# A two-layer decoder trunk on one core: the second chunk's unit 1 ahead of the first chunk's unit 3 in the first output pair

## The chip, the core and the metric

The kernel runs on one core of a Trainium2 chip. Its engines are PE (TensorE, the matmuls; PEld is its weight load), DVE (VectorE), ACT (ScalarE), POOL (GpSimd) and SP (SyncE, which only issues transfers here). The metric is the time of one execution on the device in microseconds (us).

## The reference

Two layers on x of 256 positions by 2048 columns, all in float32, cut to what matters here:

```
for l in range(2):
  h = rms_norm(x, mix_norm[l])
  q, k, v, uv, gate_logits = split(h @ w_in[l])
  branch_a = sliding_window_attention(q, k, v, sinks[l]) @ w_attn_branch[l]
  branch_b = chunked_sgu(gelu(uv), ...) @ w_sgu_branch[l]
  gates = sigmoid(gate_logits)
  merged = gates[..., :2048] * branch_a + gates[..., 2048:] * branch_b
  x = x + merged @ w_out[l]
  h2 = rms_norm(x, ffn_norm[l])
  x = x + (silu(h2 @ w_gate[l]) * (h2 @ w_up[l])) @ w_down[l]
```

The change lies at `merged @ w_out` and at the norm that follows it, in both layers.

## The kernel before

**Products.** Columns are worked in chunks of 512 (`CW`). An activation that is multiplied is first turned, so that its columns lie on the partitions, and split into a high and a low part (`uh`, `ul`); one turned chunk of 512 columns is a *unit*. A weight piece (`raw`, 256 rows by 512 columns, 512 KB) is split in the same way: ScalarE makes `whi` (L225), VectorE `wlo` (L226). `add_product` (L306) multiplies high by high, high by low and low by high.

**Entries.** `entries` is the order written out by hand in which PE takes the weight pieces; `step` (L317) takes one. A full entry (tags X, G, U) is 12 products over both halves of the positions. A pair of chunks (`pair`, L124) saves products on unit 0 (`WINO` = 0) by the Strassen-Winograd scheme: seven half entries P1 to P7 of six products, which use four sums of the unit (`sh`, `sl`) as well as the unit itself. P1 uses the unit, P5, P6, P7 and P3 the sums. A pair is a head (P1, P5, P2, P6, P7, P4) and a body. In the texts below g2 to g7 are the body's entries for the first chunk (units 1, 2 and 3, two entries each; `g[0]` to `g[5]` in the code), u2 to u7 those for the second chunk. The body before is g2, g3, g4, P3, g5, g6, g7, u2, ..., u7. The first chunk is finished by its last g entry (`on_a`), the second by the last entry (`on_b`). The head of the next pair is put between the last six body entries of a pair:

```
order = [t[0], h[0], t[1], h[1], t[2], t[3], h[3], h[2], t[4], h[4], t[5], h[5]]
```

Here t are the last six body entries, and h0, h1, ... below are the head entries of the pair that follows. In layers 0 and 1 the output projection is two pairs, ("mix", l), and the first ffn pair follows them.

**Ticks.** `after(n, fn)` (L243) puts work off by n ticks. A tick comes after a full entry, or after every second half entry (`debt`, L349). What runs at a tick is traced there; PE's instructions keep the order in which they are traced. The other engines' order is laid out when the kernel is built, by a scheduler that models the time; VectorE's instructions of a tick stand behind the weight split that was traced last (`issue_after`). A weight piece is loaded seven entries ahead (`W_LOAD`), on SyncE's queue, and split four entries ahead (`W_SPLIT`), into four buffers.

**Merging.** For each of the four chunks j, lines 926 and 928 merge the branches into `ga`. The merged chunk is then turned and split by `transposed` (L393). For the last one (j = 3) the turn is made on PE (L425), three ticks after the merge is traced; it becomes unit 3 of the output projection.

**Residual and norm.** When an output chunk j is finished, `residual` (L849) adds it to `xs` (L857), and two ticks later `nxt.unit(j)` turns it for the ffn norm, whose scale per position is applied after the products. `turn` (L376) does this for all but the last chunk: VectorE transposes blocks of 32 by 32 into `box` (one buffer), for one half of the positions at a time, one tick apart (L383), and 16 transfers of 32 KB, the gather, put the blocks in place in `tt` (L388). They are issued by GpSimd, except in attention, where they are on SyncE's queue. Unit 0 of the ffn norm then takes six steps at the ticks of `WINO_NORM` after its turn began: two scaled copies (L452), the split of the unit (L456, L457), the four sums in two steps (L471), and the split of the sums (L456, L457).

Of the kernel before, what the change touches and what calls it, by code (L numbers as in the profile page):

```python
# [28 lines left out]
NCH = D // CW  # L29
EPS = 1e-6  # L30
B = 32
W_LOAD = 7
ROUNDS = ((0, 4), (4, 8), (8, 11))
WINO = 0
WINO_NORM = 7, 8, 10, 11, 12, 13
WINO_IN = 6, 7, 8, 12, 13, 14
WINO_FIRST = 6, 7, 8, 9, 10, 11
WINO_MIX = 6, 7, 9, 10, 11, 13
# [19 lines left out]
def hybrid_trunk(ctx: ExitStack, tc: tile.TileContext, x, mix_norm, w_in, q_norm, k_norm, sinks,  # L58
                 sgu_ln_g, sgu_ln_b, w_spatial, b_spatial, w_attn_branch, w_sgu_branch, w_out,
                 ffn_norm, w_gate, w_up, w_down, cosine, sine, out):  # L60
    nc = tc.nc
# [50 lines left out]
    def load_of(w, h, tag="raw"):  # L112
        raw_no[0] += 1
        return raw_no[0], w, h, tag

    def half(w, h, tag):
        ld = load_of(w, h)
        return dict(tag=tag, h=h, loads=[ld], src=ld[0])
# [2 lines left out]

        return Plan(key, [], [half(w, h, "X") for h in range(w.shape[0] // (2 * P))])

    def pair(key, wa, wb, by_unit=False):  # L124

        h1, h2 = 2 * WINO, 2 * WINO + 1
        l11, l12, l21, l22 = (load_of(w, h, t) for w, h, t in ((wa, h1, "k11"), (wb, h1, "k12"), (wa, h2, "k21"),  # L130
                                                              (wb, h2, "k22")))
        k11, k12, k21, k22 = l11[0], l12[0], l21[0], l22[0]
        rest = [h for h in range(wa.shape[0] // (2 * P)) if h // 2 != WINO]
        g, u = [half(wa, h, "G") for h in rest], [half(wb, h, "U") for h in rest]
        head = [dict(tag="P1", loads=[l11, l12], src=k11),
                dict(tag="P5", loads=[], sums=[(k11, k12, k11)], src=k11),
                dict(tag="P2", loads=[l21, l22], src=k21),
                dict(tag="P6", loads=[], sums=[(k11, k22, k11)], src=k11),
                dict(tag="P7", loads=[], sums=[(k12, k22, k12)], src=k12),
                dict(tag="P4", loads=[], sums=[(k21, k21, k11)], src=k21)]  # L140
        p3 = dict(tag="P3", loads=[], src=k22)
        body = g[:2] + [g[2], p3] + g[3:] + u
        g[1]["then"] = "open"
        if by_unit:
            body = g[:2] + [p3] + u[:2]
            g[0]["then"] = g[1].pop("then")
            for i in range(2, len(rest), 2):
                body += g[i:i + 2] + u[i:i + 2]
        return Plan(key, head, body)

    plans = []
    for l in range(DEPTH):
        wl = w_in[l]

        def of_in(kind, c):
            o = {"kv": O_KV, "q": 0, "v": O_V, "u": O_U, "gate": O_GATE}[kind] + c * CW
            return wl[:, o:o + CW]

        for f in FIRST_PART[l]:
            plans.append((single if len(f) == 1 else pair)(("in", l), *(of_in(*c) for c in f)))  # L160
        plans += [single(("att", l), w) for w in cols_of(w_attn_branch[l], NCH)]
        sgu = [single(("sgu", l), w_sgu_branch[l, :, j * CW:(j + 1) * CW]) for j in range(NCH)]
        plans += [sgu[0], pair(("in", l), of_in("gate", 5), of_in("gate", 6)), sgu[1], sgu[2],
                  single(("in", l), of_in("gate", 7)), sgu[3]]
        c_ = cols_of(w_out[l], NCH)
        plans += [pair(("mix", l), c_[j], c_[j + 1]) for j in range(0, NCH, 2)]
        for r, (f0, f1) in enumerate(ROUNDS):
            for f in range(f0, f1):
                plans.append(pair(("ffn", l), w_gate[l, :, f * CW:(f + 1) * CW], w_up[l, :, f * CW:(f + 1) * CW], f == 0))
            c_ = cols_of(w_down[l, f0 * CW:f1 * CW, :], NCH)  # L170
            plans += [pair(("hid", l, r), c_[j], c_[j + 1], j == 0) for j in range(0, NCH, 2)]
    entries = []
    for p in plans:
        if p.head:
            h, n = p.head, min(6, len(ahead.body))
            t = [entries.pop() for _ in range(n)][::-1]
# [66 lines left out]
    def after(n, fn):  # L243
        steps.append((slot_no[0] + n, fn))
# [52 lines left out]
    def banks(p, which):  # L297
        if which not in p.acc:
            other = p.paired and p.key[0] != "in" and which == "a"
            if other or p.key[0] == "in":  # L300
                odd[0] = other and not odd[0]
            pool, tag = (ps_at, "at") if other and odd[0] else (ps_acc, "acc")
            p.acc[which] = [pool.tile([P, CW], F32, tag=tag, name=nm("acc")) for _ in range(NT)]
        return p.acc[which]
# [12 lines left out]
    def step():  # L317
        e = entries[stream.at]
        p, tag = e["plan"], e["tag"]
        units = units_at[p.key]  # L320
        w = stream.next()
        if tag in "XGU":
            ps = banks(p, "b" if tag == "U" else "a")
            todo = [(ps[t], block(units, e["h"], t)) for t in range(NT)]
        else:
            sh, sl = units[WINO][2:]
            which, t, form = {"P1": ("a", 1, (0, 0)), "P2": ("a", 0, (1, 0)), "P6": ("a", 1, 1), "P7": ("a", 1, 2),
                              "P4": ("a", 1, (1, 1)), "P5": ("a", 0, 0), "P3": ("b", 0, 3)}[tag]
            todo = [(banks(p, which)[t], (sh[:, form], sl[:, form]) if isinstance(form, int)
                     else block(units, 2 * WINO + form[0], form[1]))]  # L330
        for ps, u in todo:
            add_product(p, ps, u, w, tag in ("P4", "P7"))
        a, b = p.acc.get("a"), p.acc.get("b")
        if tag == "P5":
            p.kept = slot([P, 2, CW], name="kept")
            nc.scalar.activation(p.kept[:, 1, :], a[0], AF.Copy)  # L336
            nc.scalar.activation(a[0], a[1], AF.Copy)
        elif tag in ("P6", "P7"):
            nc.vector.tensor_tensor(out=p.kept[:, int(tag == "P7"), :], in0=a[1], in1=p.kept[:, 1, :], op=ALU.add)  # L339
        if "then" in e:  # L340
            for t, ps in enumerate(banks(p, "b")):
                nc.scalar.activation(ps, p.kept[:, t, :], AF.Copy)  # L342
                p.opened.add(id(ps))
        p.left -= 1
        if e is getattr(p, "last_g", None):
            p.calls[0](a)
        if p.left == 0 and p.paired:
            p.calls[1](b)
        debt[0] += len(todo)  # L349
        if debt[0] >= 2:  # L350
            debt[0] -= 2
            if p.left or p.paired:
                tick()
# [22 lines left out]
    def turn(dst, src, queue):  # L376


        box = turned.tile([P, 4, 4, NT, B], F32, tag="box", name=nm("box"))
        iv = src.rearrange("p t (k j c) -> p t k j c", j=4, c=B)  # L380

        def blocks(t):
            nc.vector.transpose(box[:, :, :, t, :].rearrange("p j k r -> p k j r"), iv[:, t])  # L383

        def gather():
            for j in range(4):
                for i in range(4):
                    queue.dma_start(dst[j * B:(j + 1) * B, i], box[i * B:(i + 1) * B, j])  # L388

        blocks(0)  # L390
        after(1, lambda: (blocks(1), gather()))

    def transposed(units, c, src, cols=None, on_pe=False, wino=None, again=False, queue=None, late=0):  # L393

# [31 lines left out]
            return  # L428

        tt = slot([P, 4, 4, NT, B], name="tt")  # L430
        turn(tt, src, queue or nc.gpsimd)

        def blocks_of(k0):
            return lambda k, step: tt[:, :, k0 + k:k0 + k + step].rearrange("p i k t r -> p (k t) i r")
# [48 lines left out]
    class Norm:  # L483
# [12 lines left out]

        def unit(self, c, on_pe=False, again=False):
            transposed(self.units, c, xs[:, :, c * CW:(c + 1) * CW], cols=self.cols[:, 4 * c:4 * c + 4],
                       on_pe=on_pe, again=again,
                       wino=None if c != WINO or on_pe else WINO_FIRST if again else WINO_IN if self.soon else  # L500
                       WINO_NORM)

# [371 lines left out]
    for l in range(DEPTH):  # L874
# [33 lines left out]
        for j in range(NCH):  # L908
            ps = product(("att", l))
            ga = gates[j]  # L910
# [4 lines left out]
        mT = units_at["mix", l] = [None] * NCH  # L915
        nxt = Norm(ffn_cols(l))
        units_at["ffn", l] = nxt.units
        for j in range(NCH):
            if j == 1:
                projected(("gate", 5), ("gate", 6))  # L920
            if j == 3:
                projected(("gate", 7))
            ps = product(("sgu", l))
            ga, gb = gates[j], gates[NCH + j]
            for t in range(NT):
                nc.vector.scalar_tensor_tensor(out=gb[:, t, :], in0=gb[:, t, :], scalar=1.0, in1=ps[t],
                                               op0=ALU.add, op1=ALU.mult)
                nc.vector.tensor_tensor(out=ga[:, t, :], in0=ga[:, t, :], in1=gb[:, t, :], op=ALU.add)  # L928
            after(2 + (j == NCH - 1), lambda j=j, ga=ga: transposed(mT, j, ga, on_pe=j == NCH - 1,
                                                                   wino=WINO_MIX if j == WINO else None,  # L930
                                                                   late=3 if j == NCH - 2 else 0))
            tick()
# [74 lines left out]
```

## Time and profile before

| | |
|---|---|
| median of 3 runs | 2474.78 us (2472.15 to 2475.66) |
| profiled execution, its own time | 2473.06 us |
| its span in the trace | 2471.1 us |
| granted clock of TensorE | 1.000 |
| transfers | 502.54 MB, mean 203 GB/s |
| GpSimd's gathers in the span | 480 transfers of 32 KB |

The span runs from the first to the last instruction; the execution's own time is 1.96 us more. In a row of the page or of a timeline, L12 is line 12 of the kernel and `acc<-whi,uh` is the output and what it is made from. What stands in brackets is how long the engine was idle just before and what it waited for. SPq is the queue in which SyncE issues transfers; it takes them in order.

### The profile page before, as it was taken

Reading aid. Unit: us, or ns where it says so; the run is one execution under the profiler, and the core shown is the slowest. Engines: PE = TensorE matmul, PEld = TensorE weight load, DVE = VectorE, ACT = ScalarE, POOL = GpSimd, SP = SyncE. Lnnn points to the kernel's source line nnn. Section 1 sums busy time; section 2 is a strip of 40 time slices with the busy share of each in tenths; the row PEclk is TensorE's granted clock in tenths of the full one; section 3 lists DMA queues with packets and bytes.
Section 4 is the critical chain, followed back from the end, with each engine's and each line's share of the span. In section 5 each row is a group of like instructions: output and inputs, shape, how many; then the busy total and the mean of one; then the engine's idle time right before and its main releaser. Section 6 shows DMA issues by size and latency. Waiting matters only on the chain.

```text
span 2471.1 us, 31179 instructions
## 1 busy us (share of the span) xinstructions
PE 2456.6 (99%) x11088; PEld 2032.1 (82%) x11088; DVE 1925.3 (78%) x2261; ACT 1430.8 (58%) x1794; POOL 283.2 (11%) x527
## 2 busy tenths in 40 slices
PE   9999999999999999999999999999999999999999
PEld 7888888888888888888887888888888888888887
DVE  6798676887877787778887986767878777877786
ACT  5566544575655565556655665545655555655564
POOL 3100002231110111011101000021211001110110
PEclk9999999999999999999999999999999999999999
DMA  9655667576766667576757546666767566666664
GB/s 293 203 181 163 214 200 218 182 241 190 220 197 204 214 195 223 175 228 188 227 153 265 154 155 224 208 209 188 231 188 233 189 215 195 218 198 202 213 196 148
DMA packets 275662, 502.54 MB, mean 203 GB/s; under 512 B 26225, under 2 KB 36049, under 8 KB 275505
## 3 DMA queue, kind: packets, MB, share of 16 engines
q1 hardware_dynamic: 259472, 484.25, 61.8%
q0 software_dynamic: 15712, 16.01, 2.2%
q8 instruction: 87, 1.43, 0.2%
q14 instruction: 71, 0.57, 0.1%
q10 hardware_dynamic: 320, 0.27, 0.0%
HBM read 475.27 MB, written 2.10 MB: 193 GB/s over the span
## 4 chain that ended last, share of the span: by engine, by line
PE 94%; DVE 2%; DMA 1%; SPq 1%; issue 1%; ACT 0%; POOL 0%; DVEq 0%; ACTq 0%
PE acc L314 61%; PE acc L315 30%; DMA raw<-in_w_in_dram 1%; SPq L388 1%; DVE wlo L226 1%; PE po L762 1%; PE pt L425 1%; PE ppt L752 0%; PE psc L723 0%; ACT whi L225 0%; PE psg L840 0%; DVE box L383 0%; POOL rq L286 0%; DVE raw L213 0%; DVE gate L928 0%
## 5 line engine op out<-in xcount | busy, mean ns | idle before, releaser
L226 DVE TENSOR_TENSOR wlo<-raw,whi 128x1024 fp32r<-128x1024 f32 (+1 forms) x1039 | 1260.7, 1219 | 493.7 <-ACT whi L225 485.1
L225 ACT ACTIVATE whi<-raw 128x1024 fp32r<-128x1024 f32 (+1 forms) x1039 | 1098.2, 1058 | 919.4 <-PE acc L315 720.9
L314 PE MATMUL acc<-whi,uh 128*128 128x512 f32 x3114 | 1217.9, 391 | 1.2 <-ACT uh L411 1.2
L314 PE MATMUL acc<-wlo,uh 128*128 128x512 f32 x3114 | 1214.0, 390 | 2.2 <-DVE wlo L226 2.2
L315 PE MATMUL acc<-whi,ul 128*128 128x512 f32 x3114 | 1213.5, 390 | 0.0
L314 PEld LDWEIGHTS acc<-wlo,uh 128*128 128x128 f32 x3114 | 585.1, 188 | 124.9 <-DVE wlo L226 5.0
L314 PEld LDWEIGHTS acc<-whi,uh 128*128 128x128 f32 x3114 | 585.1, 188 | 121.7 <-ACT uh L411 1.8
L315 PEld LDWEIGHTS acc<-whi,ul 128*128 128x128 f32 x3114 | 584.9, 188 | 121.7 <-DVE ul L416 0.2
L388 POOL DMA_DIRECT2D tt<-box x480 | 235.2, 497 | 1714.9 <-DVE box L383 784.1
L213 DVE TENSOR_TENSOR raw<-raw,raw 128x1024 f32<-128x1024 f32 x188 | 229.2, 1219 | 1.3
L314 PE MATMUL acc<-whi,sh 128*128 128x512 f32 x376 | 147.3, 392 | 0.0
L314 PE MATMUL acc<-wlo,sh 128*128 128x512 f32 x376 | 147.1, 391 | 0.0
L315 PE MATMUL acc<-whi,sl 128*128 128x512 f32 x376 | 146.5, 390 | 0.0
L315 PEld LDWEIGHTS acc<-whi,sl 128*128 128x128 f32 x376 | 70.6, 188 | 14.7
L314 PEld LDWEIGHTS acc<-wlo,sh 128*128 128x128 f32 x376 | 70.7, 188 | 14.6 <-DVE kept L339 0.4
L314 PEld LDWEIGHTS acc<-whi,sh 128*128 128x128 f32 x376 | 70.7, 188 | 14.3
L339 DVE TENSOR_TENSOR kept<-acc,kept 128x512 f32<-128x512 f32 x94 | 64.2, 684 | 0.0
L342 ACT ACTIVATE acc<-kept 128x512 f32<-128x512 f32 x94 | 55.1, 587 | 10.8 <-DVE kept L339 10.7
L857 DVE SCALAR_TENSOR_TENSOR xs<-acc,xs 128x512 f32<-128x512 f32 (+1 forms) x66 | 41.4, 666 | 7.8 <-PE acc L315 7.8
L946 ACT ACTIVATE hid<-acc,rhalf 128x512 f32<-128x512 f32 x44 | 30.4, 690 | 21.0 <-PE acc L315 21.0
L947 DVE SCALAR_TENSOR_TENSOR hid<-hid,acc 128x512 f32<-128x512 f32 x44 | 29.6, 683 | 8.3 <-ACT hid L946 8.3
L336 ACT ACTIVATE kept<-acc 128x512 f32<-128x512 f32 x47 | 28.0, 597 | 13.2 <-PE acc L315 13.2
(135 smaller groups left out, 880.5 us busy)
## 6 DMA issues: line engine op xcount, KB each, us to landing
raw<-in_w_in_dram SPq DMA_DIRECT2D x239, 512.0 KB, 4.7
raw<-in_w_up_dram SPq DMA_DIRECT2D x176, 512.0 KB, 4.8
raw<-in_w_gate_dram SPq DMA_DIRECT2D x176, 512.0 KB, 4.3
raw<-in_w_down_dram SPq DMA_DIRECT2D x176, 512.0 KB, 4.6
raw<-in_w_out_dram SPq DMA_DIRECT2D x64, 512.0 KB, 4.8
raw<-in_w_attn_branch_dram SPq DMA_DIRECT2D x32, 512.0 KB, 5.3
raw<-in_w_sgu_branch_dram SPq DMA_DIRECT2D x32, 512.0 KB, 4.3
tt<-box POOLq DMA_DIRECT2D x480, 32.0 KB, 4.2
```

The source lines that it names most:

```text
L213: self.last = nc.vector.tensor_tensor(out=self.raws[d], in0=self.raws[x], in1=self.raws[y], op=ALU.subtract)
L225: nc.scalar.activation(hi[:, i, :], raw[:, i, :], AF.Copy)
L226: self.last = nc.vector.tensor_tensor(out=lo[:, i, :], in0=raw[:, i, :], in1=hi[:, i, :].bitcast(F32), op=ALU.subtract)
L314: nc.tensor.matmul(ps, a, part[:, kk, :], start=first and kk + n == 0, stop=False, skip_group_check=True)
L315: nc.tensor.matmul(ps, b, hi[:, kk, :], start=False, stop=kk == 1, skip_group_check=True)
L336: nc.scalar.activation(p.kept[:, 1, :], a[0], AF.Copy)
L339: nc.vector.tensor_tensor(out=p.kept[:, int(tag == "P7"), :], in0=a[1], in1=p.kept[:, 1, :], op=ALU.add)
L342: nc.scalar.activation(ps, p.kept[:, t, :], AF.Copy)
L388: queue.dma_start(dst[j * B:(j + 1) * B, i], box[i * B:(i + 1) * B, j])
L857: nc.vector.scalar_tensor_tensor(out=xs[:, t, sl], in0=sums[t][:, i * w:(i + 1) * w], scalar=scale, in1=xs[:, t, sl], op0=ALU.mult, op1=AL ...
L946: nc.scalar.activation(th, g[t], AF.Tanh, scale=norm.rh[t])
L947: nc.vector.scalar_tensor_tensor(out=th, in0=th, scalar=1.0, in1=g[t], op0=ALU.add, op1=ALU.mult)
```

## The change

It has four parts.

- In the first output pair of each layer (`last_later`, j = 0) the body becomes g2, g3, g4, P3, g5, u2, u3, g6, g7, u4, ..., u7. The last six, between which the next head is put, are then g6, g7, u4, ..., u7.
- The turn of the last merged chunk on PE is traced four ticks after its merge instead of three.
- The steps of unit 0 of the ffn norm (`WINO_NORM`) come two ticks earlier, counted from the start of its turn.
- The gather of that unit goes alternately to SyncE's queue and to GpSimd's; all others keep theirs.

In `step` the sums of the unit are now looked up only in the entries that use them; this alters no instruction.

```diff
-WINO_NORM = 7, 8, 10, 11, 12, 13
+WINO_NORM = 5, 6, 8, 9, 10, 11
...
-    def pair(key, wa, wb, by_unit=False):
+    def pair(key, wa, wb, by_unit=False, last_later=False):
...
         body = g[:2] + [g[2], p3] + g[3:] + u
         g[1]["then"] = "open"
+        if last_later:
+            body = g[:2] + [g[2], p3, g[3]] + u[:2] + g[4:] + u[2:]
...
-        plans += [pair(("mix", l), c_[j], c_[j + 1]) for j in range(0, NCH, 2)]
+        plans += [pair(("mix", l), c_[j], c_[j + 1], last_later=j == 0) for j in range(0, NCH, 2)]
...
-                    queue.dma_start(dst[j * B:(j + 1) * B, i], box[i * B:(i + 1) * B, j])
+                    q = queue if queue is not None else (nc.sync, nc.gpsimd)[i % 2]
+                    q.dma_start(dst[j * B:(j + 1) * B, i], box[i * B:(i + 1) * B, j])
...
-        turn(tt, src, queue or nc.gpsimd)
+        turn(tt, src, queue)
...
-                       on_pe=on_pe, again=again,
+                       on_pe=on_pe, again=again, queue=None if c == WINO and not again and not self.soon else nc.gpsimd,
...
-            after(2 + (j == NCH - 1), lambda j=j, ga=ga: transposed(mT, j, ga, on_pe=j == NCH - 1,
+            after(2 + 2 * (j == NCH - 1), lambda j=j, ga=ga: transposed(mT, j, ga, on_pe=j == NCH - 1,
```

More of the change, by code (lines that the diff above doesn't have):

```diff
@@ L325, in step @@
         else:
-            sh, sl = units[WINO][2:]
             which, t, form = {"P1": ("a", 1, (0, 0)), "P2": ("a", 0, (1, 0)), "P6": ("a", 1, 1), "P7": ("a", 1, 2),
                               "P4": ("a", 1, (1, 1)), "P5": ("a", 0, 0), "P3": ("b", 0, 3)}[tag]
-            todo = [(banks(p, which)[t], (sh[:, form], sl[:, form]) if isinstance(form, int)
+            todo = [(banks(p, which)[t], tuple(x[:, form] for x in units[WINO][2:]) if isinstance(form, int)
                      else block(units, 2 * WINO + form[0], form[1]))]
@@ L387, in gather, with transposed @@
                 for i in range(4):
-                    queue.dma_start(dst[j * B:(j + 1) * B, i], box[i * B:(i + 1) * B, j])
+                    q = queue if queue is not None else (nc.sync, nc.gpsimd)[i % 2]
+                    q.dma_start(dst[j * B:(j + 1) * B, i], box[i * B:(i + 1) * B, j])
         blocks(0)
         after(1, lambda: (blocks(1), gather()))
-    def transposed(units, c, src, cols=None, on_pe=False, wino=None, again=False, queue=None, late=0):
+    def transposed(units, c, src, cols=None, on_pe=False, wino=None, again=False, queue=nc.gpsimd, late=0):
         uh, ul = units[c] if again else (slot([P, 4, S], F32R, "uh"), slot([P, 4, S], F32R, "ul"))
```

## Prediction

> **What bounds the kernel now.** I read the page's table of engines first, then the waits of the matmul engine, then the timeline around those waits. One profiled execution spans 2471.1 us and took 2473.06 us as a run, 1.72 us under the median of the three runs shown, 2474.78 us.
>
> ```profile
> PE 2456.6 (99%) x11088; PEld 2032.1 (82%) x11088; DVE 1925.3 (78%) x2261; ACT 1430.8 (58%) x1794; POOL 283.2 (11%) x527
> ```
>
> PE, the matmul engine, is busy for all but 14.5 us of the span. The change adds and removes no matmul, so it can gain only PE's waits. The view of PE's waits gives them (engine, line, what it waited for: us in total, times, longest):
>
> ```profile
> PE pt L425 <- DVE gate L928: 2.9, 2, 1.4
> PE acc L314 <- DVE wlo L226: 2.2, 5, 0.6
> ```
>
> The first row lies where the change works: the transposes of the last merged chunk wait for the merge, once in each layer. The second lies in the input projection, which the diff does not touch. Here is the first stall in the timeline (start, duration, engine, line, output<-input, count):
>
> ```profile
> 460.49 0.39 PE L314 MATMUL acc<-whi,uh 128*128 128x512 f32 x1
> ...
> 463.21 0.27 PE L425 MATMUL pt<-ident,gate 128*128 128x128 f32 x1
> 464.93 0.98 PE L425 MATMUL pt<-ident,gate 128*128 128x128 f32 x7 [1.45 <-DVE gate L928]
> 465.67 0.48 PE L314 MATMUL acc<-whi,uh 128*128 128x512 f32 x1
> ```
>
> ```profile
> 1694.11 0.98 PE L425 MATMUL pt<-ident,gate 128*128 128x128 f32 x7 [1.45 <-DVE gate L928]
> ```
>
> And here are eight undisturbed transposes, in the ffn norm (the first row from the chain of waits, where a row is start, duration, what):
>
> ```profile
> 550.36 0.87 PE pt L425 x8
> ```
>
> ```profile
> 550.99 0.48 PE L314 MATMUL acc<-whi,uh 128*128 128x512 f32 x1
> ```
>
> From the first transpose to the next product takes 465.67 − 463.21 = 2.46 us. The undisturbed eight take 550.99 − 550.36 = 0.63 us. So the stall costs 2.46 − 0.63 = 1.83 us, more than the 1.45 us counted as idle, because the weight load that hides behind a matmul is exposed as well. The row at 1694.11 is its twin in layer 1, with the same 1.45 us. Together: 3.66 us. One entry (12 products) takes 463.21 − 460.49 = 2.72 us; a half entry (P1 to P7, six products) 1.36 us.
>
> **Part 1: the turn one tick later (2 + 2 in place of 2 + 1).** A tick comes after each full entry or each second half entry. Today the transposes stand behind g2, the first body entry of the first output pair; after the change they stand behind g3. PE then arrives at 463.21 + 2.72 = 465.93. What they wait for is the second half of the merge:
>
> ```profile
> 461.92 2.35 DVE L226 TENSOR_TENSOR wlo<-raw,whi 128x1024 fp32r<-128x1024 f32 x2
> 464.19 0.68 DVE L928 TENSOR_TENSOR gate<-gate,gate 128x512 f32<-128x512 f32 x1
> ...
> 466.14 1.29 DVE L408 TENSOR_TENSOR ul<-pt,uh 128x512 fp32r<-128x512 f32 x2
> ```
>
> It ends at 464.19 + 0.68 = 464.87, 1.06 us before PE would come. The merge is traced ahead of these entries in both kernels, so I take its place in VectorE's order as unchanged. Both stalls go: −3.66 us. Lower end of the gain: VectorE's order is laid out anew, and with one more weight split (2.35 / 2, some 1.17 us) ahead of the merge it is 0.1 us late, with two about 1.3 us.
>
> **Part 2: the second chunk's unit 1 ahead of the first chunk's unit 3.** The order g5, g6, g7, u2, h0, u3 becomes g5, u2, u3, g6, h0, g7. All four moved entries have twelve products and one load of 512 KB, and they exchange places among themselves, so PE's work, the number of loads and the places of the second pair's half entries stay. Cost on PE: nothing. It covers part 1: unit 3 of the merged chunks is ready at 466.14 + 1.29 = 467.43 and first read in g6:
>
> ```profile
> 475.29 0.39 PE L314 MATMUL acc<-whi,uh 128*128 128x512 f32 x1
> ```
>
> Its room is 7.86 us today. Its making comes 2.72 us later and g6 two entries later (5.44 us), which makes 10.6 us.
>
> **Part 3: unit 0 of the ffn norm.** The first chunk is finished by g7. That comes two entries and one half entry later, 6.80 us, and by ticks three later, since h0 completes a pair of half entries. The chain's waits shrink by two ticks. So its head moves by three ticks and its end by one: the last split falls behind the second pair's g6 instead of its g5. Here are the rows of before, by engine: VectorE's, GpSimd's, ScalarE's, and the products on PE that read the unit and its sums:
>
> ```profile
> 487.07 0.70 DVE L383 STREAM_TRANSPOSE box<-xs 128x512 f32<-128x512 f32 x1
> ...
> 495.62 1.23 DVE L226 TENSOR_TENSOR wlo<-raw,whi 128x1024 fp32r<-128x1024 f32 x1 [1.46 <-ACT whi L225]
> ...
> 513.13 1.22 DVE L457 TENSOR_TENSOR ul<-flat,uh 128x1024 fp32r<-128x1024 f32 x1
> 514.27 0.42 DVE L471 TENSOR_TENSOR sums<-flat 128x256 f32<-128x256 f32 x1
> ...
> 519.88 1.22 DVE L457 TENSOR_TENSOR sl<-sums,sh 128x1024 fp32r<-128x1024 f32 x1
> ```
>
> ```profile
> 488.31 4.89 POOL L388 DMA_DIRECT2D tt<-box  x10 [45.65 <-PE acc L315]
> ```
>
> ```profile
> 509.18 1.69 ACT L452 ACTIVATE flat<-tt,vcols 128x256 f32<-128x256 f32 x4
> ```
>
> ```profile
> 525.61 0.39 PE L314 MATMUL acc<-whi,uh 128*128 128x512 f32 x1
> ...
> 529.69 0.39 PE L314 MATMUL acc<-whi,sh 128*128 128x512 f32 x1
> ```
>
> At the end there is room. The sums are split by 519.88 + 1.22 = 521.10 and read at 529.69; one tick later is 523.82, which leaves 5.9 us. The unit itself (514.35, one tick later 517.07) is read at 525.61, 8.5 us. In the middle it is tighter. On the clock of before the second box transpose moves to about 494.2, into the idle 1.46 us ahead of 495.62, so it delays no weight split there; it ends near 494.9. Then sixteen pieces must land before ScalarE's copies at 509.18.
>
> **Part 4: the gather on two queues.** GpSimd issues a piece in 4.89 / 10 = 0.49 us. What one on SyncE costs is seen in attention, whose gathers are on that queue (SPq rows: issues; then landing times, first of GpSimd's gather of unit 0, then of the SyncE pieces near 106 to 116 us):
>
> ```profile
> 88.20 10.01 SPq L388 DMA_DIRECT2D tt<-box  x16
> ```
>
> ```profile
> DMA to landing us min/median/max: 2.7/3.7/4.8
> ```
>
> ```profile
> DMA to landing us min/median/max: 1.8/1.9/4.4
> ```
>
> That is 10.01 / 16 = 0.63 us a piece. From a start at 495.5 the eight on GpSimd are out at 499.4 and landed by 504.2 at the latest (4.8); the eight on SyncE are out at 500.5 and landed by 504.9 (4.4). Both are ahead of 509.18 by over 4 us: cost nothing on PE. The price is that the weight loads on SyncE queue behind its eight pieces, 8 × 0.63 = 5.0 us in each layer. In attention a hold of twice that length shows its price: ScalarE waited for the gather and for late loads, and PE hardly noticed.
>
> ```profile
> 99.64 1.15 ACT L707 ACTIVATE qT<-tt 128x512 f32<-128x512 f32 x2 [5.47 <-DMA tt<-box]
> ```
>
> ```profile
> 123.17 0.51 PE L314 MATMUL acc<-wlo,uh 128*128 128x512 f32 x1 [0.34 <-DVE wlo L226]
> ```
>
> So I bound this at 0 to 0.34 us a layer and take 0, since the hold here is half as long. Below zero I exclude: PE waits nowhere in this stretch. [...]
>
> **Sum.** −3.66 + 0 = −3.66 us: 2471.1 − 3.7 = 2467.4 us of span, about 2469.4 us for an execution like the profiled one, and 2474.78 − 3.66 = 2471.1 us against the median. That is 0.15%.
>
> **The rivals.**
>
> *The stall stays in part: the turn is not late enough.* Two more weight splits ahead of the merge leave 1.3 us of the 1.83 us a layer; gain 1.1 us, 2473.7 us. For it: two splits already stand ahead of the second half. Against it: nothing traced earlier is moved.
>
> *Late loads.* SyncE's hold delays loads until PE waits as at 123.17: 0.34 us in each layer, 2471.1 + 0.7 = 2471.8 us. For it: a hold of 5.0 us is nearly two entries. Against it: it is half of attention's.
>
> *ScalarE held by a late gather: slower.* ScalarE's copies of unit 0 stand in line ahead of weight splits. Pieces behind a weight load on SyncE wait with it until its buffer is free:
>
> ```profile
> SPq L202 <- DVE wlo L226: 1664.4, 712, 9.7
> ```
>
> The lead of the weight splits there is seen just behind the copies, on VectorE and on PE:
>
> ```profile
> 511.99 1.23 DVE L226 TENSOR_TENSOR wlo<-raw,whi 128x1024 fp32r<-128x1024 f32 x1 [0.84 <-ACT whi L225]
> ```
>
> ```profile
> 517.67 0.39 PE L314 MATMUL acc<-wlo,uh 128*128 128x512 f32 x1
> ```
>
> The split behind the copies ends at 511.99 + 1.23 = 513.22 and its first product that needs it starts at 517.67, a lead of 4.45 us. PE pays what a hold is longer than that, and the change loses once it is longer than 4.45 + 1.83 = 6.3 us. With a hold of 9.7 us, the longest wait of a weight load in the kernel, it is 5.25 − 1.83 = 3.4 us a layer: 2474.78 + 6.8 = 2481.6 us. For it: SyncE's queue is nearly always waiting for a buffer (1664.4 us in all). Against it: it needs twice the 5.47 us seen in attention.
>
> *VectorE is full behind the chain: slower.* The chain's VectorE work comes a tick later, nearer to the stretch in which splits are last:
>
> ```profile
> 526.95 1.22 DVE L226 TENSOR_TENSOR wlo<-raw,whi 128x1024 fp32r<-128x1024 f32 x1 [1.24 <-ACT whi L225]
> ```
>
> ```profile
> 537.73 2.35 DVE L226 TENSOR_TENSOR wlo<-raw,whi 128x1024 fp32r<-128x1024 f32 x2
> 539.43 0.39 PE L314 MATMUL acc<-wlo,uh 128*128 128x512 f32 x1
> ```
>
> The first of the two splits ends at 537.73 + 1.17 = 538.9, 0.53 us before its product. If unit 0's two splits (2 × 1.22 us) and its four sums (4 × 0.42 us) all pressed on into it, 4.1 − 0.53 = 3.6 us a layer would be lost against 1.83 won: 2474.78 + 3.5 = 2478.3 us. Against it: the idle 1.24 us at 526.95 lies between, and only the last split (1.22 us) comes near it.
>
> **How the numbers follow.** About 0.2% (5 us) is what a measurement of this kernel can tell from no change. Forecast 0.60; stall stays in part 0.08; late loads 0.11; ScalarE held 0.13; VectorE full 0.08. All but the fourth lie within 0.2%. The forecast is 1.3 us short of the bound on the fast side and the three runs spread over 3.5 us, so a quarter of its 0.60 may come out as faster: 0.15. Slower is the fourth case: 0.13. The rest, 0.72, is no change by that bound. The range runs from 2471.1 less two thirds of the spread, 2468.8 us, up to the VectorE rival, 2478.3 us.
>
> **What would show it.** Right: no wait of L425 for L928 in PE's waits, PE idle some 2.9 us less; the turn of the merged chunk one entry later; two copies of unit 0 without a wait for the gather; the last split of the sums over 4 us ahead of P5; SyncE's weight loads bunched behind eight pieces in each layer. Wrong: a wait of ScalarE for the gather near 505 to 515 us of over 4.45 us, or PE waiting for a weight split between 500 and 545 us, in both layers; or the L928 wait still there.

## The result and the profile after

The changed kernel takes 2469.68 us (median of 21 runs, 2467.83 to 2472.65); the kernel before, run beside it, takes 2472.87 us (21 runs, 2471.43 to 2476.25). The ratio is 0.9987, with a 95% interval of 0.9981 to 0.9993: 3.19 us less by the medians, 1.7 to 4.7 us by the interval. The forecast was 3.66 us less. It is a gain, and it lies within 0.2%. As a time the forecast was 2471.1 us, taken from a median of three runs; with 21 runs the kernel before is itself 1.91 us lower, so the difference is what to compare. The slower of the changed kernel's runs show a lower granted clock: 2468.8 us on average at 1.000 (9 runs), 2470.6 us at 0.999 (11 runs), 2472.65 us at 0.998 (one run).

The five largest rows of PE's waits in the changed kernel (its line numbers are one or two higher than before in all rows shown here):

```profile
PE acc L316 <- DVE wlo L228: 2.2, 6, 0.8
PE ppt L754 <- DVE wsT L625: 1.5, 1, 1.5
PE pwarm L274 <- DVE warm L269: 1.1, 1, 1.1
PE acc L316 <- DVE kept L340: 0.9, 2, 0.5
PE acc L316 <- ACT uh L413: 0.8, 2, 0.4
```

The row of 2.9 us, transposes waiting for the merge, is gone, in both layers. PE's idle time in the span falls from 14.5 to 11.8 us. Here is the place of the first stall in the timeline of PE, and what VectorE does for it:

```profile
468.31 0.39 PE L317 MATMUL acc<-whi,ul 128*128 128x512 f32 x1
468.54 1.03 PE L427 MATMUL pt<-ident,gate 128*128 128x128 f32 x8
469.33 0.48 PE L316 MATMUL acc<-whi,uh 128*128 128x512 f32 x1
```

```profile
466.80 0.69 DVE L930 TENSOR_TENSOR gate<-gate,gate 128x512 f32<-128x512 f32 x1
...
470.98 1.28 DVE L410 TENSOR_TENSOR ul<-pt,uh 128x512 fp32r<-128x512 f32 x2
```

The eight transposes run in one piece. The second half of the merge ends at 466.80 + 0.69 = 467.49, 1.05 us before PE comes. From the start of the product before the transposes to the start of the one behind them takes 469.33 − 468.31 = 1.02 us.

The spans of the two profiled executions, 2471.1 and 2469.3 us, differ by only 1.8 us, because the two executions differ already ahead of the change. The last merge half started at 464.19 before and at 466.80 here, 2.61 us later, though every engine has the same instructions in the same order up to there. So I compare stretches inside an execution. From the place of the old turn to the transposes of the ffn norm's last unit, on PE, it takes 87.0 us before (463.21 to 550.20, layer 1: 1692.39 to 1779.37) and 85.2 us after (468.54 less the one entry of 2.72 us, to 551.04):

```profile
468.54 1.03 PE L427 MATMUL pt<-ident,gate 128*128 128x128 f32 x8
...
551.04 1.04 PE L427 MATMUL pt<-ident,xs 128*128 128x128 f32 x8
```

That is 1.77 us in this layer; layer 1 shows the same (86.98 and 85.21 us). Together they make 3.54 us, inside the measured interval. The experiments below are read by this "stretch" as well as by their times. It repeats well: four other kernels below that leave this part as in the changed kernel (those with `w_spatial` at ticks 38, 41 twice and 42) have 85.21 or 85.22 us in both layers.

The gather and the chain of unit 0 in the changed kernel, by SyncE's queue, GpSimd, the landing times of the sixteen pieces, ScalarE, VectorE and PE:

```profile
496.35 4.97 SPq L390 DMA_DIRECT2D tt<-box  x8
501.42 0.53 SPq L204 DMA_DIRECT2D raw<-in_w_out_dram  x1
501.99 0.47 SPq L204 DMA_DIRECT2D raw<-in_w_gate_dram  x1
```

```profile
496.61 3.92 POOL L390 DMA_DIRECT2D tt<-box  x8 [51.32 <-DVE box L384]
```

```profile
DMA to landing us min/median/max: 2.2/3.2/3.8
```

```profile
510.12 1.70 ACT L454 ACTIVATE flat<-tt,vcols 128x256 f32<-128x256 f32 x4
```

```profile
524.15 1.22 DVE L459 TENSOR_TENSOR sl<-sums,sh 128x1024 fp32r<-128x1024 f32 x1
```

```profile
530.63 0.39 PE L316 MATMUL acc<-whi,sh 128*128 128x512 f32 x1
```

Eight pieces hold SyncE's queue for 4.97 us, until 501.32, and the weight loads come bunched behind them. In the kernel before, the load at 496.87 goes out 0.02 us after a weight split ends (495.62 + 1.23); here a split ends at 496.57 + 1.23 = 497.80, and the next load goes out at 501.42:

```profile
496.87 0.37 SPq L202 DMA_DIRECT2D raw<-in_w_up_dram  x1
```

```profile
496.57 1.23 DVE L228 TENSOR_TENSOR wlo<-raw,whi 128x1024 fp32r<-128x1024 f32 x1 [0.24 <-ACT whi L227]
```

The last piece has landed by 501.32 + 3.8 = 505.1; ScalarE copies at 510.12 and waits for nothing. The sums are split by 525.37, 5.3 us ahead of their reader.

### The profile page after: what moved, and what is told of

It reads as the page before. It is cut to its first block, busy times and chain, and to the rows that moved or that the text cites. A ratio compares the mean times of both kernels' runs of the same rounds, so it can differ in the third digit from the quotient of the medians.

```text
span 2469.3 us, 31203 instructions
## 1 busy us (share of the span) xinstructions
PE 2457.5 (100%) x11088; PEld 2031.2 (82%) x11088; DVE 1926.2 (78%) x2261; ACT 1431.1 (58%) x1794; POOL 276.0 (11%) x511
## 4 chain that ended last, share of the span: by engine, by line
PE 94%; DVE 2%; DMA 2%; issue 1%; SPq 1%; ACT 0%; POOL 0%; DVEq 0%; ACTq 0%
PE acc L316 61%; PE acc L317 30%; DMA raw<-in_w_in_dram 2%; DVE wlo L228 1%; PE po L764 1%; PE pt L427 0%; SPq L390 0%; PE psc L725 0%; PE ppt L754 0%; DVE raw L215 0%; ACT whi L227 0%; PE psg L842 0%; POOL rq L288 0%; DVE pr L729 0%; DVE box L384 0%
## 5 line engine op out<-in xcount | busy, mean ns | idle before, releaser
L390 POOL DMA_DIRECT2D tt<-box x464 | 228.2, 499 | 1718.8 <-DVE box L384 920.8
```

What stands on the lines that cost most here:

```text
L390: q.dma_start(dst[j * B:(j + 1) * B, i], box[i * B:(i + 1) * B, j])
```

## The experiments

**The turn alone.** The kernel before, with one number changed.

```diff
-            after(2 + (j == NCH - 1), lambda j=j, ga=ga: ...
+            after(2 + 2 * (j == NCH - 1), lambda j=j, ga=ga: ...
```

> The kernel before with one number changed: the turn of the last merged chunk is traced four ticks after its merge (2 + 2), and the old order, chain and gather stay. Theory (the whole gain is the turn, the rest is cover that isn't needed): PE's wait of L425 for L928 is gone; from the place behind g2 to the transposes of the ffn norm it takes 85.2 us in each layer, as in the changed kernel, against 87.0 before; unit 3 is ready some 5 us ahead of g6, so PE does not wait there; about 3.5 us less than before, ratio 0.9986. Rival (the new order is needed, since the later turn alone makes unit 3 late): PE waits for uh or ul at the first product of g6, and the stretch stays at 86 us or more.

Measured: 2469.54 us, ratio to before 0.9985 (0.9976 to 0.9994); stretch 85.32 and 85.30 us.

```profile
465.52 1.03 PE L425 MATMUL pt<-ident,gate 128*128 128x128 f32 x8
466.31 0.48 PE L314 MATMUL acc<-whi,uh 128*128 128x512 f32 x1
```

```profile
467.96 1.28 DVE L408 TENSOR_TENSOR ul<-pt,uh 128x512 fp32r<-128x512 f32 x2
```

One number brings 1.67 us of the 1.77 us a layer. Unit 3 is ready at 467.96 + 1.28 = 469.24; g6 follows g4, P3 and g5, which begin at 466.31 and take 6.8 us, so some 4 us are left. PE does not wait for unit 3. The new order is cover that is not needed.

**All but the turn.** The changed kernel with `2 + (j == NCH - 1)`.

> The changed kernel with the turn put back to three ticks (2 + 1); the new order, the shorter chain and the gather on two queues stay. Theory: these three are worth nothing by themselves, the wait of L425 for L928 is back with 1.4 to 1.5 us in each layer, the stretch is 87.0 us again and the time that of before (ratio 1.000, within 0.0006). Rival (order, chain or gather bring part of the gain, or cost something that the turn hid): the stretch differs from 87.0 by 0.3 us or more.

Measured: 2472.74 us, ratio 0.9995 (0.9987 to 1.0004); stretch 86.90 us in both layers. The view of PE's waits has the row again:

```profile
PE pt L427 <- DVE gate L930: 2.9, 2, 1.4
```

New order, shorter chain and split gather together are worth 0.1 us a layer; which of them brings it is not shown, since no run has the order or the chain alone. The two experiments add up to the change.

**The gather on GpSimd alone, and on SyncE alone.** The changed kernel, with the shorter chain.

```diff
-                    q = queue if queue is not None else (nc.sync, nc.gpsimd)[i % 2]
+                    q = queue if queue is not None else nc.gpsimd
```

> The changed kernel with the gather of unit 0 wholly on GpSimd, the chain still two ticks shorter. Theory (the second queue only covers the shorter chain, and there is more room than it needs): sixteen pieces from 496.6 us are out at 505 and landed by 509 to 510; ScalarE's copies come no earlier than 510 and hold it under 1 us; PE waits nowhere from 500 to 545 us; stretch 85.2 us, ratio to before 0.9986. Rival (the split of the gather is needed): the copies wait for the gather over 4.4 us or the sums come behind P5, and PE waits for a weight split or for sl; stretch 86 us or more.

Measured: 2471.37 us, ratio 0.9991 (0.9982 to 1.0000); stretch 85.90 and 85.88 us, 0.7 us a layer longer than with the split gather. The theory misses the size, and the rival misses the way: the copies do not wait for the gather. Their place in ScalarE's order is itself later, behind two more weight splits, at 514.26 for 510.12 us. So the sums are split later too (526.63 for 524.15 us), although this execution is 1.22 us ahead of the changed kernel's at the transposes, and VectorE's rows show no idle time from there to 550 us. In the timeline of PE:

```profile
538.71 0.39 PE L317 MATMUL acc<-whi,ul 128*128 128x512 f32 x1
538.93 0.39 PE L316 MATMUL acc<-whi,uh 128*128 128x512 f32 x1
539.30 0.50 PE L316 MATMUL acc<-wlo,uh 128*128 128x512 f32 x1
...
541.71 0.39 PE L317 MATMUL acc<-whi,ul 128*128 128x512 f32 x1
542.17 0.50 PE L316 MATMUL acc<-wlo,sh 128*128 128x512 f32 x1
```

Products start 0.23 us apart otherwise. Here one starts 0.37 us and one 0.46 us behind the product before it, and the products just after them are stretched too; that makes some 0.6 of the 0.7 us. PE's own waits have no row for it, since a product counts as busy for 0.39 us. The weight loads on PEld have one for each, and VectorE's rows show what they waited for:

```profile
539.30 0.19 PEld L316 LDWEIGHTS acc<-wlo,uh 128*128 128x128 f32 x1 [0.40 <-DVE wlo L228]
542.17 0.19 PEld L316 LDWEIGHTS acc<-wlo,sh 128*128 128x128 f32 x1 [0.50 <-DVE kept L340]
```

```profile
538.03 2.35 DVE L228 TENSOR_TENSOR wlo<-raw,whi 128x1024 fp32r<-128x1024 f32 x2
541.44 0.68 DVE L340 TENSOR_TENSOR kept<-acc,kept 128x512 f32<-128x512 f32 x1
```

The first is the low part of a weight (`wlo`): the first of the two splits ends about when its product starts. The second is `kept`, VectorE's step behind P6, which ends at 542.12. This is the rival "VectorE is full behind the chain", at the place that it named.

> The changed kernel with the gather of unit 0 wholly on SyncE's queue: double the hold of the weight loads, 10 us instead of 5. Theory (loads have room): ScalarE may wait 1 to 3 us for late loads, PE 0 to 0.34 us in each layer; stretch 85.2 to 85.6 us, ratio to before 0.9986. Rival (the hold of SyncE's queue is what costs, and the half of it costs already): PE waits for weight splits by 1 us or more in each layer; stretch 86 us or more.

Measured: 2470.93 us, ratio 0.9989 (0.9981 to 0.9998); stretch 85.31 us in both layers. In SyncE's queue:

```profile
494.26 10.03 SPq L390 DMA_DIRECT2D tt<-box  x16
504.38 1.56 SPq L204 DMA_DIRECT2D raw<-in_w_out_dram  x3
```

A hold of 10.03 us costs 0.1 us a layer against half of it, and with half of it the stretch (85.22 us) is no longer than with the turn alone (85.32 us), where SyncE's queue is not held at all. The rival "late loads" falls. In the times, this kernel and the one before it cannot be told apart from the changed one; in the stretch they can.

**The turn earlier.** The kernel before, with `after(2, ...)`.

> The kernel before with the turn of the last merged chunk one tick earlier (2 instead of 2 + 1), nothing else. Theory (PE stands at the transposes until VectorE's second merge half ends, whose place in VectorE's order stays): PE comes one entry, 2.72 us, earlier to the same end, so its idle time there grows from 1.45 to about 4.2 us in each layer; 5.4 us slower than before, ratio 1.0022. Rival (the wait is not for the merge itself but for what the turn's place gives VectorE to do, so that the merge moves with it): idle under 2.5 us, ratio within 0.0008 of 1.

Measured: 2482.62 us, ratio 1.0037 (1.0024 to 1.0049), 9.8 us slower by the medians. Both expected figures miss: the theory's 5.4 us lies just under the interval. In the timeline of PE:

```profile
460.64 0.39 PE L315 MATMUL acc<-whi,ul 128*128 128x512 f32 x1
462.44 0.33 PE L425 MATMUL pt<-ident,gate 128*128 128x128 f32 x1 [1.41 <-DVE gate L928]
465.31 1.76 PE L425 MATMUL pt<-ident,gate 128*128 128x128 f32 x7 [2.55 <-DVE gate L928]
466.72 0.78 PE L314 MATMUL acc<-whi,uh 128*128 128x512 f32 x1
467.29 0.63 PE L314 MATMUL acc<-wlo,uh 128*128 128x512 f32 x1
467.72 0.63 PE L315 MATMUL acc<-whi,ul 128*128 128x512 f32 x1
```

The wait is close to the 4.2 us expected: 1.41 us, one transpose, then 2.55 us, 3.96 us in all. The merge stands still and PE stands before it. But then the seven transposes take 1.76 us for 0.98, and the products start 0.43 us apart for 0.23. The stages (length, busy time of PE, PEld, DVE, ACT, POOL, granted clock, DMA share, GB/s) show the granted clock there:

```profile
460.00:465.00 5.00, 1.36 (x6) 0.67 (x4) 5.00 (x7) 1.88 (x2) 0.00 (x0) 1.00 0.88 294
465.00:470.00 5.00, 4.69 (x17) 4.06 (x18) 1.64 (x3) 1.19 (x2) 0.00 (x0) 0.66 0.64 219
470.00:480.00 10.00, 10.00 (x45) 8.26 (x44) 4.90 (x4) 4.25 (x4) 0.00 (x0) 1.00 0.37 108
```

The granted clock is 0.66 on average in the five microseconds from 465 us on, against 1.00 in the same stretch of the kernel before. From product to product the turn takes 466.72 − 460.64 = 6.08 us against 2.69 us before (3.39 more: 2.72 up to the start of the seven transposes, 0.67 of slow transposes), and the next five products lose 0.9 us. That is 4.3 us in layer 0. Layer 1, read in the same way, has 4.2 us, and the 8.5 us together lie inside the interval of 5.9 to 12.1 us. The wait of 1.45 us in the kernel before left the clock at 1.00 (460 to 465 us and 465 to 470 us). In the gather on SyncE alone a single wait of 2.24 us, in the attention of layer 1, was followed by products as slow:

```profile
1353.83 0.66 PE L754 MATMUL ppt<-ident,pr 128*128 128x128 f32 x4 [2.24 <-DVE wsT L625]
1354.24 0.64 PE L316 MATMUL acc<-whi,uh 128*128 128x512 f32 x1
1354.67 0.63 PE L316 MATMUL acc<-wlo,uh 128*128 128x512 f32 x1
```

The products start 0.43 us apart until 1357.66, which loses some 1.6 us. The same wait in the kernel before, 2.15 us, left the clock at 1.00 (1353 to 1358 us), with products 0.23 us apart. What decides between the two is not shown.

**The turn later still.** The changed kernel with `2 + 3 * (j == NCH - 1)`.

> The changed kernel with the turn one tick later still (2 + 3). Theory (one tick takes the whole stall, and unit 3 has over 10 us of room): nothing more is won or lost, no wait at L425 or at g6, stretch 85.2 us, ratio to before 0.9986. Rival (what is left of the stall hides in stretched products, or unit 3 becomes late): stretch under 84.9 us, or over 85.6 us.

Measured: 2468.99 us, ratio 0.9986 (0.9977 to 0.9995); stretch 85.21 us in both layers. One tick took the whole stall.

**The same remedy elsewhere.** PE's other waits at transposes, in the changed kernel. First the turn of `w_spatial` (`after(40, pl.spatial)`) at tick 41.

> The changed kernel with the same remedy at the other place where PE waits for VectorE at a transpose: the turn of w_spatial is traced at tick 41 instead of 40 of a layer, so that the transposes of the attention weights (L754) no longer come right behind it for the same PSUM buffers. Theory (a turn put one tick later is free wherever its result has room): the wait of L754 for wsT (1.5 to 2.2 us in layer 1) is gone, total about 1.5 to 2 us below the changed kernel, ratio to before 0.9979 to 0.9980. Rival (VectorE's copies meet other work one tick later and give a new wait): PE idle in layer 1's attention as before, ratio 0.9986.

Measured: 2470.99 us, ratio 0.9992 (0.9983 to 1.0001): the rival. The wait for `wsT` is gone from PE's waits, and the one for `kept` has grown from 0.9 us to:

```profile
PE acc L316 <- DVE kept L340: 2.0, 2, 1.5
```

With unit 1 of layer 1's input norm one tick later besides:

```diff
-                after(3 if j == NCH - 1 and not nxt.soon else 2, lambda: nxt.unit(...
+                after(3 if j == (1 if nxt.soon else NCH - 1) else 2, lambda: nxt.unit(...
```

> The kernel of the run before this one (w_spatial at tick 41) with, besides, unit 1 of layer 1's input norm turned three ticks after its chunk instead of two; PE's wait of L427 for L859 (0.27 us idle, about 0.5 us with the stretched products) lies there. Theory: that wait goes as well, 0.5 us less, ratio to before 0.9977 to 0.9978. Rival (unit 1 is needed at once): PE waits for uh of that unit at the first product that reads it, 1 us or more lost.

Measured: 2469.91 us, ratio 0.9989 (0.9980 to 0.9998). The wait for `xs` is gone from the view, as the theory has it; the wait for `kept` stays, so the figure is missed. Then that kernel with `w_spatial` at tick 38 and at tick 42:

> The changed kernel with unit 1 of layer 1's input norm turned one tick later (as in the last kernel with w_spatial at tick 41) and the turn of w_spatial two ticks earlier, tick 38 instead of 40. Theory (a turn on PE costs nothing where VectorE has neither to free PSUM for the next transposes nor to give up a slot that PE waits for): no wait of L754 for wsT, no new wait for kept in attention, 2.5 us under the changed kernel, ratio to before 0.9977. Rival (VectorE in attention has no free slot, so the two copies of 1.28 us only move the wait): 1 us or more of PE idle comes back under another name, ratio 0.9982 to 0.9988.

> As the run before, but with the turn of w_spatial at tick 42. Theory and rival as there: 0.9977 if PE finds no wait for kept and none for wsT; 0.9982 to 0.9988 if the wait only changes its name, as at tick 41.

Measured: at tick 38 2466.57 us, ratio 0.9976 (0.9966 to 0.9985); at tick 42 2469.77 us, 0.9985 (0.9976 to 0.9994). PE's waits at tick 38, in full:

```profile
PE acc L316 <- DVE wlo L228: 1.7, 4, 0.6
PE pwarm L274 <- DVE warm L269: 1.1, 1, 1.1
PE acc L316 <- DVE kept L340: 1.0, 2, 0.5
PE acc L316 <- ACT uh L413: 0.9, 1, 0.9
PE psc L725 <- DVE att L768: 0.7, 1, 0.7
```

And at tick 42, the row that came back, now in layer 0:

```profile
PE ppt L754 <- DVE wsT L625: 1.7, 1, 1.7
```

At tick 38 the theory came true: the wait for `wsT` is gone and the one for `kept` is as in the changed kernel. At ticks 41 and 42 one of the two is there, as the rival has it. The version at tick 38, which also has the later unit 1, has the lowest time of all kernels here, 3.1 us under the changed kernel's median. Its interval and the changed kernel's (0.9981 to 0.9993) overlap, so against the change that gain is likely and not shown; against the kernel before it is shown.

## Why the prediction was right

*The sum.* The path was right: the two stalls at the last merged chunk's turn are the gain, and the turn alone takes them (1.67 us a layer by itself, the rest 0.1 us). The predicted 1.83 us a layer is 0.16 us too large, and the step that was off is the yardstick. I took the undisturbed transposes' start from a row of the chain of waits, 550.36, which begins when the chain enters them. The timeline has their start at 550.20, so they take 0.79 us and not 0.63. From product to product it is 2.69 us with the stall and 1.02 us without: 1.67 us. That is 0.22 us more than the idle 1.45 us, and the weight load, which the prediction named as the cause, goes with a small part of it. The load of the seven transposes starts with them at 464.93, where an undisturbed one starts 0.23 us ahead (549.97 for 550.20):

```profile
464.93 0.75 PEld L425 LDWEIGHTS pt<-ident,gate 128*128 128x128 f32 x7 [1.80 <-DVE gate L928]
```

```profile
549.97 1.02 PEld L425 LDWEIGHTS pt<-ident,xs 128*128 128x128 f32 x8
```

From the first of the seven to the product behind them it takes 465.67 − 464.93 = 0.74 us, for 0.68 us undisturbed: 0.06 us. The other 0.16 us is how the trace counts: the transpose ahead of the wait is busy for 0.27 us, and undisturbed the next one starts (1.04 − 0.27) / 7 = 0.11 us behind.

*Part 1.* The merge's place in VectorE's order stayed; its spare time is 1.05 us for 1.06 predicted. The rival "the stall stays in part" did not come.

*Part 2.* Room of unit 3: it is ready at 470.98 + 1.28 = 472.26. That is later than worked out, since VectorE now takes a weight split ahead of it, and g6 starts, behind g4, P3, g5, u2 and u3, at 481.67:

```profile
481.67 0.39 PE L316 MATMUL acc<-whi,uh 128*128 128x512 f32 x1
```

That leaves 9.4 us for the 10.6 worked out: right in kind, 1.2 us off. That this part is cover was said; that the cover isn't needed is shown by the turn alone.

*Parts 3 and 4.* The pieces were landed by 505.1 (predicted 504.9), and ScalarE waited for nothing. The sums had 5.3 us (predicted 5.9). The hold of the weight loads shows no cost on PE, as taken; twice the hold costs 0.1 us a layer, inside the bound of 0.34 us.

*The rivals.* "ScalarE held by a late gather" did not come in any run. With the gather on GpSimd alone the copies' place in ScalarE's order had moved back by two weight splits; with the gather on SyncE alone it had moved ahead by one, and they did not wait there either. That place is laid out when the kernel is built, and I had kept it fixed in this rival. Nor do the pieces wait behind a weight load in the changed kernel: the load ahead of them goes out at 495.73, and the first piece at 496.35, 0.03 us after the second box transpose ends (495.62 + 0.70):

```profile
495.73 0.37 SPq L204 DMA_DIRECT2D raw<-in_w_out_dram  x1
```

```profile
495.62 0.70 DVE L384 STREAM_TRANSPOSE box<-xs 128x512 f32<-128x512 f32 x1
```

"VectorE is full behind the chain" is real. It takes 0.7 us a layer when the gather is on GpSimd alone. The split gather keeps it off, and the gather on SyncE alone does so too, but for 0.1 us. So it is the use of SyncE's queue that pays for the shorter chain, and the prediction gave that queue no worth of its own.

What stays open: 0.35 us lie between 3.54 us by the stretches and 3.19 us by the medians, less than the interval can tell.

## What to carry to other kernels

Where PE is busy for 99% of the span, list its waits and price each from the product before to the product behind, against the same turn undisturbed in the same view; the idle time that is shown is too small (1.45 us here for a stall of 1.67), and delays of 0.14 and 0.23 us a product (0.37 and 0.46 us for 0.23) showed in the waits of the weight loads alone, in the run with the gather on GpSimd. A step traced by hand on the busy engine can go one slot later for free, as the turn did here, but the slot has to be tried: the same remedy only moved a wait at another place, and an earlier slot removed it. Change one number before reordering around it: here it alone brought all but 0.1 us a layer.

## What the runs showed of the hardware

Waits on PE cost more than their length here: 1.67 us for 1.45. Behind 1.41 and 2.55 us of waiting with one transpose between (the turn earlier), the granted clock was 0.66 over the five microseconds from 465 us on, with products 0.43 us apart for 0.23. One wait of 2.24 us was followed by the same slow products in one execution (the gather on SyncE alone), while 2.15 us at the same place in another, and 1.45 us elsewhere (both in the kernel before), left the clock at 1.00. And the start of one and the same order of instructions varies: the last merge half began at 464.19 us in one profiled execution and at 466.80 us in another, so a gain of 3 us is not to be read from two spans.
